# Moving the finish and the start of each FFN row group off the boundary between groups, in an eight-core decoder block

## Chip, cores and metric

The kernel runs on all 8 cores of one Trainium2 chip (two dies, cores 0 to 3 and 4 to 7). The time of a run is the device time of its slowest core, in microseconds (us). The chip has two states with this program: in some executions the cores of one die, or of both, get a lower TensorE clock and the run is several per cent longer. Such runs are called slow here; only fast runs are compared, and when a profile fell in the slow state I compare only the cores of the other die.

## The reference, cut to what matters

The model is one decoder block in float32: two kinds of sequence mixer, then a dense SwiGLU feed-forward part (FFN), each between two RMS norms. Only the FFN is touched. With `x1` the rows after the mixer:

```python
def rms_norm(x, w):
    return x * lax.rsqrt(jnp.mean(x * x, axis=-1, keepdims=True) + 1e-6) * w

# D_MODEL = 2048, D_FF = 5632; 2048 rows per core      (condensed by me)
h  = rms_norm(x1, w_pre_ffn)
ff = (silu(h @ w_gate) * (h @ w_up)) @ w_down
y  = x1 + rms_norm(ff, w_post_ffn)
```

## The kernel before

Each core works through its 2048 rows in four groups of 512. A group has a start (load four tiles of 128 rows, 1 MiB each, norm them, transpose them into `h2`), a gate and up stage (11 blocks, each with one load of `w_gate` and one of `w_up`, 2 MiB each as they land), a down stage (8 blocks with one load of `w_down` each), and a finish (norm of the result, residual load, add, store). The weights are float32 in memory and become bf16 in the load.

```python
ff = [sb(f"ff{i}", [128, D], F32, ph) for i in range(4)]      # start AND finish use these
xt = [sb(f"xq{j}", [128, D], F32, ph) for j in range(2)]
for tgi in range(NT // TG):                                   # 4 groups
    for j4 in range(4):                                       # start: load and norm
        xs, xb = ff[j4], f"ff{j4}"
        P.dma("sp", xs[:], x1d[ti * 128:(ti + 1) * 128, :], xb, r=["x1d"], w=[xb])
        P.act(junk[:], xs[:], AF.Square, ...)                 # ... root, reciprocal
        P.act(xs[:], xs[:], AF.Copy, ..., scale=...)
    for kc in range(16):                                      # start: transposes
        for j4 in range(4):
            P.tr(ps[bk][:, j4 * 128:(j4 + 1) * 128], ff[j4][:, kc * 128:(kc + 1) * 128], ident, ...)
        # eviction, 512 wide, by VectorE and ScalarE in turn:
        P.ts(h2[:, kc, :], ps[bk][:, :], wcol, None, ALU.mult, ..., w=["h2"])
    for blk in range(11):                                     # gate and up
        P.dma("pool", wslot(gsl), w_gate_v[:, :, blk * 512:(blk + 1) * 512], ...)
        P.dma("pool", wslot(usl), w_up_v[:, :, blk * 512:(blk + 1) * 512], ...)
        # ... 4 x (16 gate + 16 up matmuls), silu, product into hid
    for db in range(8):                                       # down
        P.dma("pool", dslot(ds_), w_down_v[:, :, db * 256:(db + 1) * 256], ...)
        # ... 4 x 44 matmuls, evicted into ff
    for j4 in range(4):                                       # finish
        P.dma("sp", xt[k2][:], x1d[ti * 128:(ti + 1) * 128, :], xb, r=["x1d"], w=[xb])
        # ... norm of ff[j4] (ScalarE, VectorE), then
        P.tt(xt[k2][:], xt[k2][:], ff[j4][:], ALU.add, ..., eng="pool")     # GpSimd
        P.dma("sp", y[ti * 128:(ti + 1) * 128, :], xt[k2][:], xb, r=[xb], w=["y"])
```

An eviction is the copy of a finished result out of PSUM, the memory that TensorE writes, into a tile; PSUM is used here in banks of 512 columns (`ps`).

A list scheduler orders the instructions of each engine by estimated costs when the kernel is built, and every engine then runs its list strictly in order. Waits come from tracked names: an instruction that writes a name waits for the one that wrote it before.

## Time and profile before

| | before |
|---|---|
| three timed runs | 7005.32, 6694.4, 7066.68 us (one fast, two slow) |
| profiled run | 6699.66 us, fast; cores 6653 to 6698 us |
| FFN, first gate matmul to last matmul, mean of cores | 2233.7 us |
| of it: four gate stages / four down stages / three gaps between groups | 1223.8 / 807.2 / 202.6 us |

The lower two rows are my tabulation from TensorE's timelines of all eight cores: a gate stage runs from its first to its last matmul, a down stage from the last gate matmul to the last down matmul (so the wait for its first weights is in it), the gap from the last down matmul to the next gate matmul.

### The profile page before, as it was taken

How to read it: one execution, taken by the hardware profiler on the slowest of the kernel's cores; microseconds unless marked ns; L12 is line 12 of the kernel's file. 1: busy time of each engine (PE TensorE's matmuls, PEld its weight loads, DVE VectorE, ACT ScalarE, POOL GpSimd, SP SyncE). 2: the span in 40 equal slices, each digit the busy share in tenths (PEclk: the TensorE clock that was granted, in tenths of full speed). 3: DMA queues.
4: the chain of work that ended last, by engine and by line, in shares of the span. 5: the costliest groups of instructions: out<-in, count | busy, mean ns of one | idle time of the engine just before them, and what ended most of it. 6: DMA issues, size and time to landing. Idle time of an engine off the chain costs nothing. (4 is left out here: it accounts for less than half of the span.)

```text
span 6698.1 us, 76172 instructions; the slowest of 8 cores (6653.1 to 6698.1 us)
## 1 busy us (share of the span) xinstructions
PE 4857.1 (73%) x26232; PEld 2606.6 (39%) x26232; DVE 2288.5 (34%) x4634; ACT 2138.4 (32%) x3524; POOL 361.9 (5%) x218
## 2 busy tenths in 40 slices
PE   5885788589735667565546654969859886986987
PEld 3443444344322333232222221434644473464446
DVE  1346235522731555577766541210010001001001
ACT  5631552264142545544444541220020002002000
POOL 0000000000000000000000000310010011001001
PEclk8997999699867868676668877989979998997999
DMA  5122122221023110212132344499899898988988
GB/s 128 26 44 45 76 38 41 60 73 29 13 82 73 31 36 15 49 37 61 42 70 53 79 94 103 152 168 153 107 170 144 118 127 166 155 110 164 151 117 135
DMA packets 514618, 591.83 MB, mean 88 GB/s; under 512 B 14880, under 2 KB 465568, under 8 KB 495392
## 3 DMA queue, kind: packets, MB, share of 16 engines
q0 software_dynamic: 444928, 356.66, 38.1%
q1 hardware_dynamic: 69312, 230.30, 10.8%
q8 instruction: 217, 3.56, 0.2%
q14 instruction: 161, 1.32, 0.1%
HBM read 888.77 MB, written 54.79 MB: 141 GB/s over the span
## 5 line engine op out<-in xcount | busy, mean ns | idle before, releaser
L272 PE MATMUL ps<-h_s,wr_s 128*128 128x512 bf16 x5632 | 1223.8, 381 | 12.8 <-ACT h_s L287 11.5
L272 PE MATMUL ps<-hT_s,wb_s 128*128 128x512 bf16 x2816 | 702.0, 411 | 197.5 <-DVE ub_s L315 90.1
L272 PE MATMUL ps<-hTp_s,wbp_s 128*128 128x512 bf16 x3456 | 790.5, 388 | 69.5 <-DVE ubp_s L315 30.6
L272 PEld LDWEIGHTS ps<-h_s,wr_s 128*128 128x128 bf16 x5632 | 552.5, 98 | 683.1 <-issue 24.3
L272 PE MATMUL ps<-wr_s,hid_s 128*128 128x256 bf16 x5632 | 656.8, 282 | 168.5 <-DMA wr_s<-w_down 168.5
L272 PEld LDWEIGHTS ps<-wr_s,hid_s 128*128 128x128 bf16 x5632 | 568.4, 101 | 257.8 <-issue 174.8
L272 PEld LDWEIGHTS ps<-hTp_s,wbp_s 128*128 128x128 bf16 x3456 | 342.0, 100 | 485.7 <-issue 113.3
L272 PEld LDWEIGHTS ps<-hT_s,wb_s 128*128 128x128 bf16 x2816 | 287.9, 104 | 602.1 <-issue 340.0
L296 DVE TENSOR_TENSOR hid_s<-sg_s,ps 128x512 bf16<-128x512 f32 x176 | 120.9, 687 | 1112.0 <-PE ps L272 1112.0
L287 ACT ACT_TABLE_LOAD x287 | 368.2, 1283 | 409.6 <-PE ps L272 178.0
L287 ACT ACTIVATE sg_s<-ps 128x512 f32<-128x512 f32 x176 | 105.1, 597 | 1081.9 <-PE ps L272 1081.9
L272 PE MATMUL ps<-wbp_s,hTp_s 128*128 128x512 bf16 x1536 | 358.6, 394 | 59.0 <-ACT hTp_s L287 23.2
L276 PE MATMUL ps<-cst_s,T_s 128*128 128x128 f32 (+1 forms) x1200 | 197.3, 312 | 152.5 <-ACT T_s L287 79.1
L272 PE MATMUL ps<-hT_s,mixT_s 128*128 128x512 bf16 x1024 | 223.1, 381 | 79.2 <-DMA hT_s<-w_out 79.2
L315 DVE COPY ff_s<-ps 128x256 f32<-128x256 f32 x64 | 27.1, 424 | 741.1 <-PE ps L272 741.1
L272 PEld LDWEIGHTS ps<-wbp_s,hTp_s 128*128 128x128 bf16 x1536 | 153.5, 101 | 253.9 <-issue 89.6
L314 ACT ACTIVATE ff_s<-ps 128x256 f32<-128x256 f32 x64 | 24.5, 383 | 706.6 <-PE ps L272 706.6
L287 ACT ACTIVATE T_s<-T_s 128x2048 f32<-128x2048 f32 (+1 forms) x75 | 142.9, 1905 | 296.6 <-DVE T_s L305 247.1
L276 PEld LDWEIGHTS ps<-cst_s,T_s 128*128 128x128 f32 (+1 forms) x1200 | 157.1, 163 | 192.9 <-issue 185.8
L301 DVE TENSOR_SCALAR xwt_s<-ps,wst_s 128x64 bf16<-128x64 f32 x768 | 186.0, 280 | 76.4 <-PE ps L276 47.7
L305 DVE SCALAR_TENSOR_TENSOR T_s<-ubp_s,pp_s,T_s 128x2048 f32<-128x2048 f32 x90 | 210.3, 2342 | 0.1
L276 PE MATMUL ps<-cst_s,ff_s 128*128 128x128 f32 x256 | 43.0, 324 | 205.7 <-ACT ff_s L287 199.5
(227 smaller groups left out, 5422.1 us busy)
## 6 DMA issues: line engine op xcount, KB each, us to landing
wr_s<-w_gate POOLq DMA_DIRECT2D x44, 2048.0 KB, 17.6
wr_s<-w_up POOLq DMA_DIRECT2D x44, 2048.0 KB, 25.2
wr_s<-w_down POOLq DMA_DIRECT2D x32, 2816.0 KB, 23.3
T_s<-xpre SPq DMA_DIRECT2D x48, 1024.0 KB, 9.2
wbp_s<-w_in POOLq DMA_DIRECT2D x21, 2048.0 KB, 15.1
wb_s<-w_in POOLq DMA_DIRECT2D x13, 2048.0 KB, 18.2
xt_s<-xin SPq DMA_DIRECT2D x17, 1024.0 KB, 7.0
abc_s<-acsd SPq DMA_DIRECT2D x64, 256.0 KB, 3.9
```

What stands on the lines that cost most here:

```text
L272: return self.op("pe", lambda e: e.matmul(out, lhsT, rhs, start=start, stop=stop), r, w, stop if inc is None else inc, cost=c)
L276: return self.op("pe", lambda e: e.transpose(out, in_, ident), r, w, inc, cost=110.0)
L287: return self.op(eng, lambda e: e.activation(out, in_, func, **kw), r, w, cost=c)
L296: return self.op(eng, lambda e: e.tensor_tensor(out, in0, in1, op), r, w, cost=self._dc(out, 2, eng))
L301: return self.op(eng, lambda e: e.tensor_scalar(out, in0, s1, None, op0), r, w, cost=c)
L305: return self.op("dve", lambda e: e.scalar_tensor_tensor(out, in0, scalar, in1, op0, op1), r, w, cost=self._dc(out, 2))
L314: return self.op("act", lambda e: e.activation(out, in_, AF.Copy), r, w, cost=220.0 + 0.85 * self._n(out))
L315: return self.op(eng, lambda e: e.tensor_copy(out, in_), r, w, cost=self._dc(out, 1, eng))
```

## The change

Its intent is to let TensorE go from one group's down stage straight into the next group's gate stage. Loads and norm of the next group get tiles of their own (`xa`) and run in two rounds of two row tiles under the down stage; the finish of the old group is spread over the next gate stage, one row tile at each of blocks 2, 4, 6 and 8. Three state tiles of an earlier phase are freed to make room. `u.preds` are the instructions that `u` waits for, `u.cost` is only the list scheduler's estimate of how long it takes. The diff, cut to its core:

```diff
+            xa = [sb(f"xa{j}", [128, D], F32, ph) for j in range(2)]
...
+            def post(tgi, j4, after):                      # the finish of one row tile
+                u = P.dma("sp", xt[k2][:], x1d[ti * 128:(ti + 1) * 128, :], xb, r=["x1d"], w=[xb])
+                u.preds.update(after)                       # not before these weights have landed
+                if after:
+                    u.cost = 40000.0
+                ...                                         # as before: norm, add on GpSimd, store
+            def pre_tile(tgi, rnd, jj):
+                if tgi == 0 and rnd == 0:
+                    return ff[jj], f"ff{jj}"
+                return xa[jj], f"xa{jj}"
...
             for tgi in range(NT // TG):
-                for j4 in range(4):
-                    xs = ff[j4]
+                for rnd in range(2):
+                    for jj in range(2):
+                        xs, xb = pre_tile(tgi, rnd, jj)     # load, norm as before
...
-                        P.ts(h2[:, kc, :], ps[bk][:, :], wcol, None, ALU.mult, ..., w=["h2"])
+                            o_ap = h2[:, kc, rnd * 256:(rnd + 1) * 256]      # half as wide
+                            i_ap = ps[bk][:, kk2 * 256:(kk2 + 1) * 256]
+                            if kk2 == 0:
+                                P.ts(o_ap, i_ap, wcol, None, ALU.mult, ..., w=[h2n])
+                            else:
+                                P.act(o_ap, i_ap, AF.Copy, ..., w=[h2n], scale=wcol)
...
-                    P.dma("pool", wslot(gsl), w_gate_v[...], ...)
-                    P.dma("pool", wslot(usl), w_up_v[...], ...)
+                    ug = P.dma("pool", wslot(gsl), w_gate_v[...], ...)
+                    uu = P.dma("pool", wslot(usl), w_up_v[...], ...)
+                    if tgi > 0 and blk in (2, 4, 6, 8):
+                        post(tgi - 1, blk // 2 - 1, [ug, uu])
...
-                for j4 in range(4):                         # the finish at the group's end
-                    ...
+                if tgi == NT // TG - 1:
+                    for j4 in range(4):
+                        post(tgi, j4, [])
```

More of the change, by code (lines that the diff above doesn't have):

```diff
@@ L374, in build @@
         lbc = sb("lbc", [128, 16], F32)
-        Sinb = sb("Sinb", [128, HK, 128], BF16)
-        SinA = sb("SinA", [128, 8, 128], BF16)
-        SinB = sb("SinB", [128, 8, 128], BF16)
+        sinst = ExitStack()
+        Sinb = sb("Sinb", [128, HK, 128], BF16, sinst)
+        SinA = sb("SinA", [128, 8, 128], BF16, sinst)
+        SinB = sb("SinB", [128, 8, 128], BF16, sinst)
         ps = [es.enter_context(nc.psum_tensor(f"ps{i}", [128, 512], F32)) for i in range(8)]
@@ L1226, in build @@
         mid.close()
+        sinst.close()
         with ExitStack() as ph:
@@ L1230, in build @@
             pw1 = sb("pw1", [128, D], F32, ph)
-            h2 = sb("h2", [128, 16, TG], BF16, ph)
+            h2s = [sb("h2", [128, 16, TG], BF16, ph)] * 2
             hid = sb("hid", [128, 44, TG], BF16, ph)
@@ L1235, in build @@
             xt = [sb(f"xq{j}", [128, D], F32, ph) for j in range(2)]
+            xa = [sb(f"xa{j}", [128, D], F32, ph) for j in range(2)]
             sg = [sb(f"sg{j}", [128, TG], F32, ph) for j in range(2)]
             junk = sb("junk5", [128, D], BF16, ph)
+            pjunk = [junk[:, 0:1024], junk[:, 1024:2048]]
             st = sb("st5", [128, 16], F32, ph)
+            st6 = sb("st6", [128, 16], F32, ph)
             w_gate_v = w_gate.rearrange("(k p) n -> p k n", p=128)
@@ L1248, in dslot @@
                 return wr[:, 2 * i:2 * i + 2, :].rearrange("p a b -> p (a b)")[:, 0:44 * 256].rearrange("p (f n) -> p f n", n=256)
-            for tgi in range(NT // TG):
-                for j4 in range(4):
-                    ti = tgi * 4 + j4
-                    xs = ff[j4]
-                    xb = f"ff{j4}"
-                    P.dma("sp", xs[:], x1d[ti * 128:(ti + 1) * 128, :], xb, r=["x1d"], w=[xb])
-                    ss = st[:, 4 * j4:4 * j4 + 1]
-                    P.act(junk[:], xs[:], AF.Square, r=[xb], w=["junk5", f"st5{j4}"], accum_out=ss)
-                    P.ts(st[:, 4 * j4 + 1:4 * j4 + 2], ss, 1.0 / D, EPS, ALU.mult, ALU.add, r=[f"st5{j4}"], w=[f"st5{j4}"])
-                    P.act(st[:, 4 * j4 + 2:4 * j4 + 3], st[:, 4 * j4 + 1:4 * j4 + 2], AF.Sqrt, r=[f"st5{j4}"], w=[f"st5{j4}"])
-                    P.recip(st[:, 4 * j4 + 3:4 * j4 + 4], st[:, 4 * j4 + 2:4 * j4 + 3], r=[f"st5{j4}"], w=[f"st5{j4}"])
-                    P.act(xs[:], xs[:], AF.Copy, r=[xb, f"st5{j4}"], w=[xb], scale=st[:, 4 * j4 + 3:4 * j4 + 4])
-                for kc in range(16):
-                    bk = kc % 4
-                    for j4 in range(4):
-                        P.tr(ps[bk][:, j4 * 128:(j4 + 1) * 128], ff[j4][:, kc * 128:(kc + 1) * 128], ident,
-                             r=[f"ff{j4}", "cst"], w=[f"ps{bk}"], inc=(j4 == 3))
-                    wcol = pp[:, C_PREFFN + kc:C_PREFFN + kc + 1]
-                    if kc % 2 == 0:
-                        P.ts(h2[:, kc, :], ps[bk][:, :], wcol, None, ALU.mult, r=[f"ps{bk}", "pp"], w=["h2"])
-                    else:
-                        P.act(h2[:, kc, :], ps[bk][:, :], AF.Copy, r=[f"ps{bk}", "pp"], w=["h2"], scale=wcol)
@@ new lines, in post @@
+            def post(tgi, j4, after):
+                ti = tgi * 4 + j4
+                k2 = j4 % 2
+                xb = f"xq{k2}"
+                u = P.dma("sp", xt[k2][:], x1d[ti * 128:(ti + 1) * 128, :], xb, r=["x1d"], w=[xb])
+                u.preds.update(after)
+                if after:
+                    u.cost = 40000.0
+                ss = st[:, 4 * j4:4 * j4 + 1]
+                P.act(junk[:], ff[j4][:], AF.Square, r=[f"ff{j4}"], w=["junk5", f"st5{j4}"], accum_out=ss)
+                P.ts(st[:, 4 * j4 + 1:4 * j4 + 2], ss, 1.0 / D, EPS, ALU.mult, ALU.add, r=[f"st5{j4}"], w=[f"st5{j4}"])
+                P.act(st[:, 4 * j4 + 2:4 * j4 + 3], st[:, 4 * j4 + 1:4 * j4 + 2], AF.Sqrt, r=[f"st5{j4}"], w=[f"st5{j4}"])
+                P.recip(st[:, 4 * j4 + 3:4 * j4 + 4], st[:, 4 * j4 + 2:4 * j4 + 3], r=[f"st5{j4}"], w=[f"st5{j4}"])
+                P.stt(ff[j4][:], ff[j4][:], st[:, 4 * j4 + 3:4 * j4 + 4], pw1[:], ALU.mult, ALU.mult,
+                      r=[f"ff{j4}", f"st5{j4}", "pw1"], w=[f"ff{j4}"])
+                P.tt(xt[k2][:], xt[k2][:], ff[j4][:], ALU.add, r=[xb, f"ff{j4}"], w=[xb], eng="pool")
+                P.dma("sp", y[ti * 128:(ti + 1) * 128, :], xt[k2][:], xb, r=[xb], w=["y"])
@@ new lines, in pre_tile @@
+            def pre_tile(tgi, rnd, jj):
+                if tgi == 0 and rnd == 0:
+                    return ff[jj], f"ff{jj}"
+                return xa[jj], f"xa{jj}"
+            for tgi in range(NT // TG):
+                h2 = h2s[tgi % 2]
+                h2n = "h2"
+                for rnd in range(2):
+                    for jj in range(2):
+                        j4 = rnd * 2 + jj
+                        ti = tgi * 4 + j4
+                        xs, xb = pre_tile(tgi, rnd, jj)
+                        P.dma("sp", xs[:], x1d[ti * 128:(ti + 1) * 128, :], xb, r=["x1d"], w=[xb])
+                        ss = st6[:, 4 * j4:4 * j4 + 1]
+                        P.act(junk[:], xs[:], AF.Square, r=[xb], w=["junk6", f"st6{j4}"], accum_out=ss)
+                        P.ts(st6[:, 4 * j4 + 1:4 * j4 + 2], ss, 1.0 / D, EPS, ALU.mult, ALU.add, r=[f"st6{j4}"], w=[f"st6{j4}"])
+                        P.act(st6[:, 4 * j4 + 2:4 * j4 + 3], st6[:, 4 * j4 + 1:4 * j4 + 2], AF.Sqrt, r=[f"st6{j4}"], w=[f"st6{j4}"])
+                        P.recip(st6[:, 4 * j4 + 3:4 * j4 + 4], st6[:, 4 * j4 + 2:4 * j4 + 3], r=[f"st6{j4}"], w=[f"st6{j4}"])
+                        P.act(xs[:], xs[:], AF.Copy, r=[xb, f"st6{j4}"], w=[xb], scale=st6[:, 4 * j4 + 3:4 * j4 + 4])
+                    for k2_ in range(8):
+                        bk = k2_ % 4
+                        for kk2 in range(2):
+                            kc = 2 * k2_ + kk2
+                            for jj in range(2):
+                                P.tr(ps[bk][:, (kk2 * 2 + jj) * 128:(kk2 * 2 + jj + 1) * 128], pre_tile(tgi, rnd, jj)[0][:, kc * 128:(kc + 1) * 128], ident,
+                                     r=[pre_tile(tgi, rnd, jj)[1], "cst"], w=[f"ps{bk}"], inc=(kk2 == 1 and jj == 1))
+                        for kk2 in range(2):
+                            kc = 2 * k2_ + kk2
+                            wcol = pp[:, C_PREFFN + kc:C_PREFFN + kc + 1]
+                            o_ap = h2[:, kc, rnd * 256:(rnd + 1) * 256]
+                            i_ap = ps[bk][:, kk2 * 256:(kk2 + 1) * 256]
+                            if kk2 == 0:
+                                P.ts(o_ap, i_ap, wcol, None, ALU.mult, r=[f"ps{bk}", "pp"], w=[h2n])
+                            else:
+                                P.act(o_ap, i_ap, AF.Copy, r=[f"ps{bk}", "pp"], w=[h2n], scale=wcol)
@@ L1272, in build @@
                 for blk in range(11):
                     gsl, usl = (blk % 2) * 2, (blk % 2) * 2 + 1
-                    P.dma("pool", wslot(gsl), w_gate_v[:, :, blk * 512:(blk + 1) * 512], f"wr{gsl}", w=[f"wr{gsl}"])
-                    P.dma("pool", wslot(usl), w_up_v[:, :, blk * 512:(blk + 1) * 512], f"wr{usl}", w=[f"wr{usl}"])
+                    ug = P.dma("pool", wslot(gsl), w_gate_v[:, :, blk * 512:(blk + 1) * 512], f"wr{gsl}", w=[f"wr{gsl}"])
+                    uu = P.dma("pool", wslot(usl), w_up_v[:, :, blk * 512:(blk + 1) * 512], f"wr{usl}", w=[f"wr{usl}"])
@@ L1281, in build @@
                             P.mm(ga[:, :], wslot(gsl)[:, kc, f4 * 128:(f4 + 1) * 128], h2[:, kc, :],
-                                 start=(kc == 0), stop=(kc == 15), r=[f"wr{gsl}", "h2"], w=[f"ps{k2}"])
+                                 start=(kc == 0), stop=(kc == 15), r=[f"wr{gsl}", h2n], w=[f"ps{k2}"])
                         for kc in range(16):
                             P.mm(ua[:, :], wslot(usl)[:, kc, f4 * 128:(f4 + 1) * 128], h2[:, kc, :],
-                                 start=(kc == 0), stop=(kc == 15), r=[f"wr{usl}", "h2"], w=[f"ps{2 + k2}"])
+                                 start=(kc == 0), stop=(kc == 15), r=[f"wr{usl}", h2n], w=[f"ps{2 + k2}"])
                         P.act(sg[k2][:], ga[:, :], AF.Silu, r=[f"ps{k2}"], w=[f"sg{k2}"])
@@ L1298, in build @@
                              eng=("act" if j4 % 2 else "dve"))
-                for j4 in range(4):
-                    ti = tgi * 4 + j4
-                    k2 = j4 % 2
-                    xb = f"xq{k2}"
-                    P.dma("sp", xt[k2][:], x1d[ti * 128:(ti + 1) * 128, :], xb, r=["x1d"], w=[xb])
-                    ss = st[:, 4 * j4:4 * j4 + 1]
-                    P.act(junk[:], ff[j4][:], AF.Square, r=[f"ff{j4}"], w=["junk5", f"st5{j4}"], accum_out=ss)
-                    P.ts(st[:, 4 * j4 + 1:4 * j4 + 2], ss, 1.0 / D, EPS, ALU.mult, ALU.add, r=[f"st5{j4}"], w=[f"st5{j4}"])
-                    P.act(st[:, 4 * j4 + 2:4 * j4 + 3], st[:, 4 * j4 + 1:4 * j4 + 2], AF.Sqrt, r=[f"st5{j4}"], w=[f"st5{j4}"])
-                    P.recip(st[:, 4 * j4 + 3:4 * j4 + 4], st[:, 4 * j4 + 2:4 * j4 + 3], r=[f"st5{j4}"], w=[f"st5{j4}"])
-                    P.stt(ff[j4][:], ff[j4][:], st[:, 4 * j4 + 3:4 * j4 + 4], pw1[:], ALU.mult, ALU.mult,
-                          r=[f"ff{j4}", f"st5{j4}", "pw1"], w=[f"ff{j4}"])
-                    P.tt(xt[k2][:], xt[k2][:], ff[j4][:], ALU.add, r=[xb, f"ff{j4}"], w=[xb], eng="pool")
-                    P.dma("sp", y[ti * 128:(ti + 1) * 128, :], xt[k2][:], xb, r=[xb], w=["y"])
+                if tgi == NT // TG - 1:
+                    for j4 in range(4):
+                        post(tgi, j4, [])
             P.flush()
```

## The prediction

> **What bounds the kernel now.** The change touches only the last phase, the FFN, which works through four groups of 512 rows. I read the cores' spans first (6653 to 6698 us, granted clocks 0.841 to 0.845: both dies undisturbed, so this is the fast state). Two of the three timed runs before, 7005 and 7067 us, are 5 to 6% longer than the third, 6694; I take them for the slow state and work from 6694.4 and the profiled 6699.7, so from 6,697.
>
> Next I read TensorE's waits over the FFN (engine, line, waited for: us in total, times, longest).
>
> ```profile
> PE ps L276 <- ACT ff_s L287: 199.5, 4, 53.0
> PE ps L272 <- DMA wr_s<-w_down: 168.5, 22, 21.1
> PE ps L272 <- ACT h_s L287: 11.5, 4, 3.0
> ```
>
> The first line is the transposes (L276) waiting until ScalarE has normalised the next group's rows; the second is the down projection waiting for weights. TensorE's timeline shows where they fall (start, length, instruction, idle before).
>
> ```profile
> 4869.58 40.69 PE L272 MATMUL ps<-wr_s,hid_s 128*128 128x256 bf16 x352 [6.87 <-DMA wr_s<-w_down]
> 4917.45 21.43 PE L272 MATMUL ps<-wr_s,hid_s 128*128 128x256 bf16 x176 [7.19 <-DMA wr_s<-w_down]
> 4991.78 6.60 PE L276 MATMUL ps<-cst_s,ff_s 128*128 128x128 f32 x36 [52.90 <-ACT ff_s L287]
> ...
> 5007.26 305.61 PE L272 MATMUL ps<-h_s,wr_s 128*128 128x512 bf16 x1408 [2.88 <-ACT h_s L287]
> 5332.95 41.10 PE L272 MATMUL ps<-wr_s,hid_s 128*128 128x256 bf16 x352 [20.08 <-DMA wr_s<-w_down]
> ```
>
> From the end of one down projection (4938.88) to the next gate matmul (5007.26) are 68.4 us. The same reading at the other two boundaries gives 68.0 (5526.02 to 5594.05) and 62.8 (6106.16 to 6168.99): 199.2 us in all. The gap before group 0 and the tail after group 3 (6673.2 to 6698.1) are no boundaries of this kind. The gate and up stage runs without a break, 11 blocks in 305.6 us; between its regular issues a block takes 27.65 us. The chain of waits says what fills the gap:
>
> ```profile
> 4925.16 2.01 ACT junk_s L287 x2
> 4927.50 1.28 ACT L287
> 4929.37 2.36 DVE ff_s L305
> 4931.93 4.51 POOL xq_s L296
> 4936.53 8.65 DMA y<-xq_s
> 4945.63 17.02 DMA xq_s<-x1d
> 4962.85 4.49 POOL xq_s L296
> 4967.83 13.94 DMA ff_s<-x1d
> 4981.86 2.01 ACT junk_s L287 x2
> ```
>
> The finish of the old group (norm, residual add, store) and the start of the new one follow each other because both use the four ff tiles. Twelve 1 MiB tiles move here: four stores, four residual loads, four loads to normalise. So the gap is not only latency, it is also busy with transfers. The table by windows, one stretch each for gate and up, down, the gap, and the first two blocks after it (busy by engine, granted clock, DMA share, GB/s), decides how free their new place is:
>
> ```profile
> 4535.00:4562.00 27.00, 27.00 (x127) 12.23 (x126) 2.75 (x4) 2.21 (x4) 1.69 (x2) 1.00 1.07 155
> 4752.00:4772.00 20.00, 20.00 (x174) 17.39 (x173) 0.85 (x2) 0.38 (x1) 0.00 (x0) 0.94 0.01 2
> 4939.00:5007.00 68.00, 10.99 (x64) 9.26 (x64) 13.50 (x22) 26.45 (x31) 15.49 (x5) 0.60 1.00 256
> 5007.00:5033.00 26.00, 25.74 (x113) 11.37 (x114) 2.06 (x3) 3.08 (x5) 0.00 (x0) 0.93 0.00 1
> 5034.00:5061.00 27.00, 27.00 (x127) 12.21 (x125) 2.75 (x4) 1.87 (x4) 2.08 (x2) 1.00 1.05 156
> ```
>
> The transfers are as full in the gate stage (1.05) as in the gap. They idle for the first block after a gap, because two blocks of weights landed inside it, and during the first down block (0.01). TensorE and the transfers are nearly balanced; a change that only moves transfers has little room.
>
> **What the Trainium skill says.** "DMA: Bandwidth & Descriptors", section "Issuing engines are not separate DMA queues": transfers issued by any engine end up on the same 16 DMA engines and interleave. The trace agrees: an up weight load that lands after 25 us in the gate stage took 59.9 us when issued in the gap, beside the tiles. So moving the tiles to SyncE's issue under the gate stage doesn't make them free. The same page, "Queues, rings and completion order", says that each engine takes turns between queues by packet. Here a packet of the tiles' queue averages 7.3 KB (46.02 MB in 6323), of the weights' queue 0.76 KB (276.26 MB in 361810): a tile should get through and the weights pay. "SBUF — State Buffer", section "SBUF: two separate sides", describes an exclusive port lock between VectorE with two SBUF inputs and GpSimd. The trace fits: the 128x2048 scaling took 2.35 us alone and 5.75 beside GpSimd's add. "ScalarE: Activation LUTs", section "What ACT_TABLE_LOAD costs", gives about 1283 ns for a load; the trace has 1283.
>
> **The change part by part.** (1) Loads and norm of the next group go to two new tiles (xa), in two rounds of two row tiles, and no longer need ff. The built order places round 0's 32 transposes ahead of the first down matmul, round 1's as 16 after 88 down matmuls and 16 after 88 more. The gap's 52.9 us wait for ff and the transposes after it leave the boundary. (2) The finish of the old group is spread over the next gate stage, one row tile at each of blocks 2, 4, 6 and 8, whose residual load waits until that block's weights have landed. (3) Evictions get half as wide and twice as many. Freeing the Sin tiles only makes room.
>
> Removed: 68.4 + 68.0 + 62.8 = 199.2 us.
>
> Given back in the down stage. Round 0's transposes take about 7 us (40 took 7.08 at the full rate; eviction paces them at about 0.8 us a bank) and lie inside the 20 us for which TensorE waits for the first w_down load anyway: free. At about +7 us they release xa, and two tile loads join that w_down load. A tile costs 35.7 / 12 = 2.97 us of all engines (the tile queue held 52.5% of the 68 us gap), so the first down block starts some 5.5 us later. Round 1 then needs squares, root and scaling, 4 x 2 us plus about 1.3, after loads landing near +21: ready at about +31, before 88 matmuls (10 us) are done at +36. No stall. Its 32 transposes add about 7 us on TensorE, and as the third w_down load is issued when the first down block ends, they delay it: 12.5 us so far. Then two more tile loads, for the group after next, compete with that third load. That could be 6 us; some is absorbed, as the load waits for TensorE elsewhere, so I take 2.5. Sum 15 us after groups 0 and 1, and 8 after group 2, where no such loads follow: 38 us.
>
> Given back in the gate stage. When it is backlogged, the weight pair of a block takes 26.1 us (ups landing at 4456.5, 4482.9, 4508.3 and 4534.7), so 1.55 us per block are left of 27.65. The up load lands some 3.8 us before it is needed (landed 5061.3, needed 5065). Each finished row tile moves two tiles, 5.9 us, per two blocks, against 3.1 us of room. Step by step: the lead of about 3 us leaves 1.3 us of stall at the first, then about 2.9 at each of three: 10 us per stage, in three stages 30 us. At the start of the stage the first up pair lands about 26.1 us after the last w_down load (4917.3 + 26.1 = 4943.4; needed 4938.9 + 3.6): 1 us, three times 3 us.
>
> Net: 199.2 - 38 - 30 - 3 = 128 us. 6,697 - 128 = 6,569, called 6,570: 1.9% faster.
>
> **The rivals.** (A) All hidden: the tiles run in holes of the transfers, the stage does not stall, and the down stage grows by 5 us each: 199 - 20, about 6,515. For it: the idle first block and first down block, shares of 1.16 early in group 0 without a stall. Against: that idle first block disappears with the gap that paid for it. (B) Saturated transfers: all 23.8 us of tiles in a gate stage become stalls, and GpSimd's add, which stands in the same queue ahead of block 4's weight issues, sometimes holds them back because its residual tile is late. A tile landed after 7.5 to 17 us, the add takes 4.5, and the next issue is about 24 us away: it just fits, but 5 us more per tile would cost 20 us per stage. Then 199 - 38 - 3 - 71 - up to 60: 6,610 to 6,670. (C) ScalarE in order: in the down stage the squares for the group after next stand ahead of an eviction and wait for a load, so one of two banks stays full. I work out about 5 us of stall, ending when the third w_down load lands, thus hidden; with loads of 17 us, 5 to 8 us would show twice.
>
> **Range and chances.** In the fast state I expect 6,500 to 6,650. A gain of 2% needs 134 us, 6 more than my sum, and second-order costs tend to be missed: faster 0.42, within 2% 0.56, slower 0.02. The upper end is set at 6,890, because two of three runs before were slow ones and a median may fall there; the 6,570 is meant for fast runs.
>
> **What would show it.** TensorE's 53 us waits for ff must be gone and the next gate matmul must follow the down stage within about 3 us. The down stages should be about 222, 227 and 214 us (207, 212, 206 before), the later gate stages about 316 (305.6). The waits should show w_up or w_gate with some 30 us. I am wrong if the gate stages stay at 306 (then 6,540 or less), if they pass 330, if TensorE waits for evictions or for xa, or if GpSimd's weight issues wait for an add.

## More of the kernel before

The main views are shown in the prediction. Two more are needed later. The first fence holds lines of the page of the kernel before, first its span, then three rows of its table of transfers (what is loaded from what, issuing engine, count, KB each, median us from issue to landing).

```profile
span 6698.1 us, 76172 instructions; the slowest of 8 cores (6653.1 to 6698.1 us)
...
wr_s<-w_gate POOLq DMA_DIRECT2D x44, 2048.0 KB, 17.6
wr_s<-w_up POOLq DMA_DIRECT2D x44, 2048.0 KB, 25.2
wr_s<-w_down POOLq DMA_DIRECT2D x32, 2816.0 KB, 23.3
```

The second is one row of the table by windows (length, busy time by engine, granted clock, DMA share, GB/s) over most of a gate stage, ten blocks on the slowest core.

```profile
5034.00:5310.00 276.00, 276.00 (x1281) 125.15 (x1279) 27.49 (x40) 23.67 (x40) 22.41 (x19) 1.00 1.01 148
```

TensorE is busy for all of the 276 us, and the DMA share already reads 1.01. The up load lands 25.2 us after its issue, and a block lasts 27.65. Both are close to full; whatever is added to this stage has to fit in what is left.

## The result and the profile after

| | before | after |
|---|---|---|
| median of all runs | 6977.06 us (15 runs) | 6790.1 us (12 runs) |
| fast runs | 6693.71, 6694.4, 6698.31, 6702.26 | 6583.52, 6588.98, 6592.25, 6592.8 |
| ratio of fast runs | | 0.9839, 95% interval 0.9822 to 0.9856 |

A ratio is the mean time of one kernel's fast runs over the mean of the other's fast runs of the same rounds, so it is not quite the ratio of the medians quoted beside it. The change makes fast runs 1.6% or 108 us faster. The profiled run after was fast (6592.25 us, slowest core 4).

Lines of the page after that answer to those of before:

```profile
span 6590.4 us, 76090 instructions; the slowest of 8 cores (6534.7 to 6590.4 us)
...
wr_s<-w_gate POOLq DMA_DIRECT2D x44, 2048.0 KB, 26.9
wr_s<-w_up POOLq DMA_DIRECT2D x44, 2048.0 KB, 35.3
wr_s<-w_down POOLq DMA_DIRECT2D x32, 2816.0 KB, 23.3
```

Gate and up loads take 9 to 10 us longer from issue to landing, though their number and size are the same. TensorE's waits over the FFN on core 4 (waited for: us in total, times, longest) show what that costs:

```profile
PE ps L272 <- DMA wr_s<-w_down: 160.8, 20, 23.6
PE ps L272 <- DMA wr_s<-w_up: 44.5, 13, 6.5
PE ps L276 <- ACT st_s L287: 41.8, 1, 41.8
```

The three waits of 53, 53 and 48 us at the boundaries are gone; the 41.8 us are the start of group 0, which was there before. The wait for `w_down` is as before. New is the wait for `w_up`: 44.5 us in 13 pieces. TensorE's timeline (start, length, instruction, idle before and what ended it) shows one boundary and the gate stage after it:

```profile
4938.94 20.71 PE L272 MATMUL ps<-wr_s,hid_s 128*128 128x256 bf16 x176 [5.43 <-DMA wr_s<-w_down]
4959.70 89.73 PE L272 MATMUL ps<-h_s,wr_s 128*128 128x512 bf16 x407
5051.78 55.41 PE L272 MATMUL ps<-h_s,wr_s 128*128 128x512 bf16 x251 [2.34 <-DMA wr_s<-w_up]
5112.41 57.06 PE L272 MATMUL ps<-h_s,wr_s 128*128 128x512 bf16 x251 [5.22 <-DMA wr_s<-w_up]
5171.62 55.41 PE L272 MATMUL ps<-h_s,wr_s 128*128 128x512 bf16 x251 [2.14 <-DMA wr_s<-w_up]
5230.76 50.19 PE L272 MATMUL ps<-h_s,wr_s 128*128 128x512 bf16 x219 [3.73 <-DMA wr_s<-w_up]
```

The gate stage now follows the down stage without a gap (4959.65 to 4959.70). Once per two blocks, which is once per finished row tile, TensorE waits 2 to 5 us for an up load.

On core 4 that is nearly all of it. The other cores show one more wait: about 7 us after its first matmul a stage needs its first up load, and at 14 of the 24 boundaries (three on each of eight cores) TensorE waits for it, up to 6.1 us; the means over the cores are 1.6, 2.9 and 1.9 us for groups 1, 2 and 3. On core 2, 12 us after the first matmul of the stage (4931.39):

```profile
4943.41 84.37 PE L272 MATMUL ps<-h_s,wr_s 128*128 128x512 bf16 x376 [5.16 <-DMA wr_s<-w_up]
```

The stage of core 4 by windows:

```profile
4959.70:5280.79 321.09, 306.18 (x1380) 138.27 (x1408) 34.69 (x48) 32.81 (x52) 43.09 (x25) 0.99 1.11 168
```

TensorE's busy time is 306 us, that of a whole stage before; the other 15 are waits. The transfers move 168 GB/s where they moved 148, and the DMA share reads 1.11, so the 1.01 of before was not a ceiling.

The ledger, as the mean of eight cores from TensorE's timelines ("start" is from the last matmul of the phase before to the first gate matmul):

| us | before | after | difference |
|---|---|---|---|
| start of group 0 | 59.1 | 63.5 | +4.4 |
| gate stage of group 0 | 306.5 | 306.2 | -0.3 |
| gate stages of groups 1, 2, 3 | 305.4, 305.7, 306.2 | 323.1, 325.8, 329.9 | +17.7, +20.1, +23.7 |
| down stages of groups 0, 1, 2 | 200.0, 206.4, 202.3 | 217.1, 213.9, 209.5 | +17.1, +7.5, +7.2 |
| down stage of group 3 and tail | 224.2 | 223.6 | -0.6 |
| three gaps | 202.6 | 0 | -202.6 |

The sum is -105.8 us; the mean span of the cores fell by 104.8 (6673.3 to 6568.5), since the phases before the FFN ended about 1 us later. So 202.6 us went away and 98 came back: 61.5 in gate stages, 31.8 in down stages, 4.4 at the start.

### The profile page after: what moved, and what is told of

Read it like the earlier page. It is cut to its first block, busy times and chain, and to the rows that moved or that the text cites. A ratio compares the mean times of both kernels' runs of the same rounds, so it can differ in the third digit from the quotient of the medians.

```text
span 6590.4 us, 76090 instructions; the slowest of 8 cores (6534.7 to 6590.4 us)
## 1 busy us (share of the span) xinstructions
PE 4830.9 (73%) x25887; PEld 2602.3 (39%) x26232; DVE 2283.3 (35%) x4666; ACT 2157.0 (33%) x3564; POOL 362.4 (5%) x218
## 5 line engine op out<-in xcount | busy, mean ns | idle before, releaser
L272 PE MATMUL ps<-h_s,wr_s 128*128 128x512 bf16 x5516 | 1231.2, 383 | 55.2 <-DMA wr_s<-w_up 44.5
L272 PE MATMUL ps<-hTp_s,wbp_s 128*128 128x512 bf16 x3375 | 774.6, 386 | 77.4 <-DVE xwt_s L301 30.8
L315 DVE COPY ff_s<-ps 128x256 f32<-128x256 f32 x64 | 27.2, 424 | 624.4 <-PE ps L272 624.4
L309 DVE TENSOR_TENSOR_SCAN T_s<-cst_s,T_s 128x2048 f32<-128x2048 f32 (+1 forms) x27 | 119.5, 4424 | 180.8 <-ACT T_s L287 180.5
## 6 DMA issues: line engine op xcount, KB each, us to landing
wr_s<-w_up POOLq DMA_DIRECT2D x44, 2048.0 KB, 35.3
wbp_s<-w_in POOLq DMA_DIRECT2D x21, 2048.0 KB, 15.3
```

Source lines behind the costliest of these rows:

```text
L272: return self.op("pe", lambda e: e.matmul(out, lhsT, rhs, start=start, stop=stop), r, w, stop if inc is None else inc, cost=c)
L309: return self.op("dve", lambda e: e.tensor_tensor_scan(out, d0, d1, init, op0, op1), r, w, cost=100.0 + 2.1 * self._n(out))
L315: return self.op(eng, lambda e: e.tensor_copy(out, in_), r, w, cost=self._dc(out, 1, eng))
```

## The experiments

The theory I tested, called T, is that in the gate stages each 1 MiB tile takes time from the weight loads, so that the stall is the tiles' and nothing else's. Rivals were O, the order of the matmuls (from group 1 on the built order after is gate, gate, up, up where it was gate, up, gate, up), and Q, GpSimd's in-order queue, in which the add stands ahead of the next weight issue. The trace alone speaks against Q in this kernel. These are two lines of GpSimd's timeline on core 4, the add of a row tile and the next weight issue:

```profile
5088.74 4.50 POOL L296 TENSOR_TENSOR xq_s<-xq_s,ff_s 128x2048 f32<-128x2048 f32 x1 [14.12 <-DMA xq_s<-x1d]
5094.00 1.18 POOL L328 DMA_DIRECT2D wr_s<-w_gate  x1 [0.76 <-PE ps L272]
```

After the add the issue still waits, for TensorE to free the slot (0.76 us here; 2.48, 3.22 and 0.87 at the other three of this stage). The add held nothing back, but 0.76 is a thin margin. It is the same on the other cores: in 92 of the 96 cases the issue after the add waits for TensorE, and in the other four it follows the add within 0.1 us, with the next up issue at the usual 6.9 us behind it.

"Gates" below are the stages of groups 1 to 3, "downs" those of groups 0 to 2, both as means of the cores. Experiments 1 to 4 ran on one chip, where the kernel before took 6702.99 us; the others on another, where its fast runs took 6697 to 6725 us. Every stage time is from one profiled run. The gate stage of group 0, which no edit but that of 9 and 11 touches, took 305.8 to 307.8 us in them (306.2 after), so the chips can be compared in this.

### 1. No residual loads (result wrong on purpose)

```diff
-                u = P.dma("sp", xt[k2][:], x1d[...], xb, r=["x1d"], w=[xb])
-                u.preds.update(after)
...
-                P.tt(xt[k2][:], xt[k2][:], ff[j4][:], ALU.add, r=[xb, f"ff{j4}"], w=[xb], eng="pool")
+                P.tt(xt[k2][:], ff[j4][:], ff[j4][:], ALU.add, r=[f"ff{j4}"], w=[xb], eng="pool")
```

> The changed kernel with the four residual loads of each finish left out (the scaled tile is added to itself, so the output is wrong on purpose); the stores stay, so four of the eight 1 MiB tiles per later gate stage go. Theory T (the gate stage is bound by what the 16 DMA engines move: 26.8 us per weight pair plus 3.05 us per tile, as the landings of the changed kernel give): gate stages 1 to 3 fall from 323 to 330 us (mean of 8 cores) to 308 to 313 us, so some 40 us off the whole kernel. Rival Q (GpSimd's add, waiting for its residual tile, holds back the weight issues behind it): 305 to 307 us, as the add then waits for nothing. Rival O (the other order of gate and up matmuls costs the time): unchanged, 323 to 330.

Measured: gates 317.4, 319.6, 317.9, fast run 6580.05 us. That is less than after, but more than expected. The edit changed more than I meant. Without the load that waited for weights, the finish was ready at once, and all four stores went out at the start of the stage; the stall (8.35 us for `w_up` on one core) sat in block 1 instead of being spread. A miss as a clean test of four tiles; experiment 10 does that better.

### 2. Each residual tile loaded twice

```diff
+                if after:
+                    u2 = P.dma("sp", xt[k2][:], x1d[ti * 128:(ti + 1) * 128, :], xb, r=["x1d"], w=[xb])
+                    u2.cost = 40000.0
```

> The changed kernel with every spread-out residual load done twice, one after the other into the same tile (right result): twelve tiles per later gate stage in place of eight. T: a pair of blocks needs 2 x 26.8 + 3 x 3.05 = 62.8 us against 59.7, four times: gate stages 1 to 3 at 335 to 342 us, kernel about 36 us longer. Q: the add is ready some 10 us later each time and holds the weights by 7 to 10 us: 350 us or more per stage. O: unchanged, 323 to 330.

Measured: gates 333.1, 333.5, 338.4 with 12, 12 and 14 tiles in the stage; fast run 6633.17 us, result correct. Ten more us for four more tiles in the first of them, about 8 in the others. Theory T holds, just under its range in two stages; an unchanged stage (O) and a jump past 350 us (Q) are ruled out. The kernel was 40 to 50 us longer than after, where 36 were expected; the downs had grown too (222.2, 221.5, 214.2).

### 3. The kernel before, with eight extra tile loads per gate stage

```diff
+                    if tgi > 0 and blk in (2, 4, 6, 8):
+                        for z in range(2):
+                            tz = tgi * 4 + blk // 2 - 1
+                            u = P.dma("sp", xz[z][:], x1d[tz * 128:(tz + 1) * 128, :], f"xz{z}", r=["x1d"], w=[f"xz{z}"])
+                            u.preds.update([ug, uu])
```

> The kernel before, with nothing of the change but eight dummy loads of 1 MiB tiles in each of gate stages 1 to 3 (two at each of blocks 2, 4, 6 and 8, released as in the changed kernel when that block's weights have landed; nobody reads them). T: gate stages 1 to 3 go from 306 us to 321 to 330 us, the 67 us gaps stay within 3 us, the kernel is 50 to 65 us longer (about 6750). Q and O: no add and no other order here, so gate stages stay at 306 us.

Measured: gates 320.0, 320.0, 319.3, gaps 68.1, 67.8, 67.2; fast run 6756.65 us, 54 us over the kernel before. This is the cleanest proof of T: old matmul order, no finish in the stage, no add on GpSimd, only the tiles, and the stage grows by 13 to 15 us, just under the range. In the first two stages it is 3 to 6 us less than in the kernel after, in part because here the first two blocks' weights still land in the gap: on no core does TensorE wait for a stage's first up load, where after it waits 1.6 and 2.9 us on average.

### 4. Only the first part of the change: the finish in one burst at the group's end

```diff
-                    if tgi > 0 and blk in (2, 4, 6, 8):
-                        post(tgi - 1, blk // 2 - 1, [ug, uu])
...
-                if tgi == NT // TG - 1:
-                    for j4 in range(4):
-                        post(tgi, j4, [])
+                for j4 in range(4):
+                    post(tgi, j4, [])
```

> The changed kernel with only the first part of the change: the next group is normalised ahead in its own tiles, but the finish of the old group is issued at the group's end as before, with nothing that holds it to blocks 2, 4, 6 and 8. T: the same eight tiles meet the same stream of weights, only all at the start; the gate stages 1 to 3 are 320 to 332 us as in the changed kernel, with the stall in the first two or three blocks. Rival S (the spreading is what makes the change work): tiles and adds bunched in front of the weights cost 340 us or more per stage, 30 us or more on the kernel beyond the changed one.

Measured: gates 328.8, 330.5, 338.8 (the last raised by two cores' 357 and 361); one run, 6655.86 us, in which die 0 had a slightly lower clock (0.839); the cores of the other die took 6569 to 6608 us, against 6557 to 6590 after. TensorE's timeline on core 5 at the start of a gate stage:

```profile
4958.98 8.48 PE L272 MATMUL ps<-h_s,wr_s 128*128 128x512 bf16 x32 [4.19 <-DMA wr_s<-w_gate]
4982.16 271.28 PE L272 MATMUL ps<-h_s,wr_s 128*128 128x512 bf16 x1248 [14.70 <-DMA wr_s<-w_up]
```

The whole stall comes first, then 271 us run unbroken. Spreading the finish, the second part of the change, is worth only about 5 us per gate stage: it moves the stall, it does not remove it. On the undisturbed die the FFN as a whole was 26 us longer than after (2151.3 against 2125.6 us), 12 of them in the gates and 15 in the downs, which vary by several us from run to run (see 8).

### 5. Both halves of a bank evicted by the same engine

```diff
-                            if kk2 == 0:
+                            if k2_ % 2 == 0:
```

This asks about the 4.4 us at the start. Two lines of the kernel before (VectorE, core 3), then two of the kernel after (ScalarE, then VectorE, core 3), all evictions into `h2`:

```profile
4418.48 0.75 DVE L301 TENSOR_SCALAR h_s<-ps,pp_s 128x512 bf16<-128x512 f32 x1 [0.94 <-ACT h_s L287]
4420.12 0.75 DVE L301 TENSOR_SCALAR h_s<-ps,pp_s 128x512 bf16<-128x512 f32 x1 [0.89 <-ACT h_s L287]
```

```profile
4414.58 0.47 ACT L287 ACTIVATE h_s<-ps,pp_s 128x256 bf16<-128x256 f32 x1 [0.75 <-DVE h_s L301]
4415.23 0.48 DVE L301 TENSOR_SCALAR h_s<-ps,pp_s 128x256 bf16<-128x256 f32 x1 [0.74 <-ACT h_s L287]
```

Each engine waits for the other's write, though they write different bytes. Before, two 512-wide evictions took 1.64 us; after, two 256-wide ones take about 1.25, so half the width costs three quarters of the time.

> The changed kernel with the transposed halves evicted by bank (VectorE takes both halves of one PSUM bank, ScalarE both of the next) in place of one half of every bank each. Theory H (the two halves of one bank are evicted one after the other by two engines, since the kernel's helper orders engines on a bank; each bank then costs about 1.2 us of TensorE's time in place of 0.9): the time from the last output-projection matmul to the first gate matmul falls from 63.5 us (mean of 8 cores) to 58 to 60 (59.1 before the change). Rival L (that time is set by the loads and the norm of four tiles in two rounds): it stays at 63 to 64. Gate and down stages within 3 us of the changed kernel's either way.

Measured: start 62.5 us (63.5 after); gates 323.5, 321.9, 326.8; fast run 6605.49 us. A miss: the change of engine inside a bank is not the cost. The evictions still take turns through the one tracked name.

### 6. The old matmul order

```diff
+                            if f4 > 0 or blk > 0:
+                                mg.preds.add(mu)          # a gate group after the up group before it
...
+                            mu.preds.add(mg)              # an up group after its gate group
```

> The changed kernel with gate and up matmuls forced into the order that the kernel before has (gate, up, gate, up); its own scheduler gives gate, gate, up, up from group 1 on. T: the first up weights are needed 3.5 us earlier and the gate slot is freed 3.5 us later, so a lead of 3 to 7 us is lost once per stage: gate stages 1 to 3 at 325 to 336 us (323 to 330 in the changed kernel). Rival O (the new order costs the time): 306 to 316 us.

Measured: slow (die 1 at 0.828), so only cores 0 to 3 (0.846): gates 326.4, 324.6, 334.6, against 322.7, 325.0, 328.7 on the same cores after. No gain, so O is out: the order is not what lengthens the stage.

### 7. Four of the eight tiles moved to the transfers' hole in the down stage

The two residual loads for row tiles 0 and 1 and the two stores for row tiles 2 and 3 are tied to the first 44 down matmuls, where the transfers were idle before (share 0.01 in the prediction's table).

```diff
+                        if db == 0 and j4 == 0:
+                            for jp in range(2):
+                                if tgi > 0:
+                                    ystore(tgi - 1, 2 + jp, [md])     # stores of row tiles 2, 3
+                                xload(tgi, jp, [md])                  # residuals of row tiles 0, 1
```

> The changed kernel with four of the eight tiles of each finish taken out of the gate stage and put where the transfers idle, the first block of the down stage (two residual loads of this group, two stores of the last one, released by the first down matmul group); output right. T: with four tiles left, spread out, 4 x 3.05 us against 9 us of room: gate stages 1 to 3 at 307 to 314 us (323 to 330), down stages 0 to 2 at most 5 us longer than 217, 214, 210, so 30 to 50 us off the kernel: about 6545, 0.5 to 0.8% faster than the changed kernel. Rival C (the transfer time is conserved, it only changes place): down stages longer by 10 to 12 us each, kernel within 15 us of 6590. Q: gate stages not under 318, as the adds stand in GpSimd's queue as before.

Measured: gates 317.1, 318.1, 318.9 with 4 tiles each, downs 217.5, 223.2, 212.7; one fast run, 6574.24 us. Better than after, but short of 307 to 314, and the second down stage grew by 9 us where at most 5 were expected. GpSimd's timeline on core 0 gives the reason:

```profile
5525.92 4.51 POOL L296 TENSOR_TENSOR xq_s<-xq_s,ff_s 128x2048 f32<-128x2048 f32 x1 [29.27 <-DMA wr_s<-w_up]
5530.37 1.18 POOL L328 DMA_DIRECT2D wr_s<-w_gate  x1
5531.55 1.16 POOL L328 DMA_DIRECT2D wr_s<-w_up  x1
```

My edit tied the add to weights that landed late, and both issues behind it start with no wait of their own: their slots were free, the gate's some 15 us earlier. After all 96 adds of the run the next issue follows without a wait of its own. Here rival Q is real, though it is not in the kernel after.

### 8. No finish in groups 0 to 2 (result wrong on purpose)

```diff
-                    if tgi > 0 and blk in (2, 4, 6, 8):
-                        post(tgi - 1, blk // 2 - 1, [ug, uu])
```

> The changed kernel without any finish for groups 0 to 2 (no residual load, no scaling, no add, no store: 12 of the 16 row tiles of the output are never written, wrong on purpose), so no tile crosses gate stages 1 to 3. It measures what those stages cost apart from the tiles. Theory R (the weights alone leave room, 26.7 us per block against 27.65): 305 to 308 us, as in group 0. Theory I (a stage that begins without the lead that the old gap gave is short by about 5 us whatever follows, which a line through the stages with 12 and 8 tiles suggests): 309 to 313 us.

Measured: gates 307.1, 304.0, 304.9 with no tiles; one fast run, 6562.08 us. TensorE's wait for `w_up`, on its slowest core:

```profile
PE ps L272 <- DMA wr_s<-w_up: 6.3, 2, 5.3
```

With the finish gone the gate stages are back at 304 to 307 us, so nearly all of the loss there belongs to the finish. What the missing gap itself costs is the wait for a stage's first up load, the only one left: 2.3, 0 and 0.7 us on average, 5.3 to 6.7 on four cores. But the downs became 220.0, 222.3, 218.6, that is 3, 8 and 9 us longer than after, and the FFN gained only 35 us (2088.5 against 2123.6) where the gates gave 63. The trace puts most of that in waits for `w_down` after the first down matmul, 21.4, 25.1, 22.0 and 18.6 us in the four groups against 20.5, 18.3, 15.3 and 15.0 after. The last group is among them, whose down stage no edit of the finish touches; over the runs with both dies undisturbed that stage took 197.8 to 204.5 us. So a few us in the downs are within what they vary by, and what sets these waits is open.

### 9. The halves of `h2` tracked under two names

```diff
-                            if kk2 == 0:
-                                P.ts(o_ap, i_ap, wcol, None, ALU.mult, ..., w=[h2n])
+                            if k2_ % 2 == 0:
+                                P.ts(o_ap, i_ap, wcol, None, ALU.mult, ..., w=["h2v"])
                             else:
-                                P.act(o_ap, i_ap, AF.Copy, ..., w=[h2n], scale=wcol)
+                                P.act(o_ap, i_ap, AF.Copy, ..., w=["h2s"], scale=wcol)
```

The matmuls then read both names.

> The changed kernel, evictions by bank as in e5, and VectorE's and ScalarE's evictions into h2 tracked under two names, so that one engine's eviction no longer waits for the other's last one. Theory W (each eviction waits for the one before it, as all write the one tracked name h2; 1.28 us per pair of halves, 16 pairs): the time from the last output-projection matmul to the first gate matmul falls from 63.5 us (mean) to 54 to 58, below the 59.1 of the kernel before. Rival L (loads and norm set it): 62 to 64. Stages 1 to 3 of the gate within 4 us of the changed kernel's.

Measured: start 55.3 us, so the serial writes were the cost: the only difference from 5 is the two names. Of the 8.2 us won there, 5.7 came back in the gate stage of group 0 (311.9 after 306.2), which now waits for weights. The later gates (325.0, 325.3, 338.8) and the time (6638.34 us) were disturbed in the last stage: two cores of die 0, which had a clock of 0.838, took 366 us in it (329.5 is the mean of the other die).

### 10. Four tiles in the down stage, and the add where it holds nothing back

As 7, but the add follows the first up matmuls of block 3, 5, 7 or 9 instead of the landing of weights:

```diff
+                        if tgi > 0 and blk in (3, 5, 7, 9) and f4 == 0:
+                            jp = blk // 2 - 1
+                            finish(tgi - 1, jp).preds.add(mu)
+                            if jp < 2:
+                                ystore(tgi - 1, jp, [])
```

> As e7, four of eight tiles in the down stage's hole, but GpSimd's add is released only one block later, when its tile has long landed, so that it cannot hold weight issues as it was seen to do in e7 (a gate load issued 15 us late). T with Q: gate stages 1 to 3 at 307 to 313 us (317 to 319 in e7), down stages as in e7 (217, 223, 213) or shorter; 6545 to 6560 us. If e7's stages came from the transfers alone: 316 to 319 again.

Measured: gates 312.2, 311.3, 313.3, downs 218.3, 219.9, 212.2; FFN 2093.3 us against 2123.6 after; one fast run, 6565.99 us, where I had expected 6545 to 6560. A gate stage after a boundary, on the slowest core:

```profile
4982.97 195.29 PE L272 MATMUL ps<-h_s,wr_s 128*128 128x512 bf16 x896 [5.34 <-DMA wr_s<-w_up]
```

After the wait for the first up load seven blocks run without a break. This confirms both halves of the reading of 7: four tiles cost about 7 us, and the late add had cost another 5 to 7 (the two stores tied to weights in 7 moved with the add). Of the 42 us that the gates are shorter than after, 10 came back in the downs.

### 11. Both: 10 and the two names

> e10 and e9 together, meant to beat both kernels: the sum of the two, 12 to 20 us less in the gate stages each, 6 to 9 us less at the start; 6535 to 6555 us, 2.2 to 2.5% under the kernel before.

The edit is the sum of 9 and 10. Measured: fast runs 6533.49, 6552.55 and 6556.42 us; ratio to the kernel before 0.9756 (0.9737 to 0.9776), so faster by 2.4%, result correct. Start 54.8, gates of all four groups 313.4, 312.7, 314.4, 313.0, downs 208.3, 212.7, 207.9. TensorE's waits over the FFN on core 0:

```profile
PE ps L272 <- DMA wr_s<-w_down: 85.1, 20, 20.0
PE ps L276 <- ACT xa_s L287: 68.0, 3, 23.3
PE ps L272 <- DMA wr_s<-w_up: 25.9, 11, 6.1
```

This is the version that beats both kernels; the kernel after did not run beside it, but its fast runs on the first chip took 6584 to 6593 us, and on this chip the kernel before is some 20 us slower (6713 to 6723 us). In the down stage the new order puts three quarters of the transposes ahead of the first down matmul; they wait for `xa` at the time when TensorE had waited for `w_down` anyway (29 us from the last gate matmul to the first down matmul, as in 10), and the downs are 4 to 10 us shorter than in 10. That the order is the cause is my reading; it was not tested by itself.

## Why the prediction was right or wrong

**The number.** For fast runs the text foresaw 128 us off (1.9%); 108 (1.6%) were measured, within 2% as it thought most likely, and the fast runs of 6584 to 6593 lie in its range for that state. Two steps failed. In the sum for fast runs it is the gate stage, the term "10 us per stage, in three stages 30 us" (33 with the 3 us of the junction), which measured 61.5; some 10 us of that miss and of the start's 4.4 were made good by luck, as the gaps were 3.4 us larger and the down stages 6.2 us cheaper than foreseen. The other is the base: 6570 is a fast-state time, and the median of the three timed runs before, over both states, is 7005. Read against that it says 6% faster, four times what the fast runs show, and it disagrees with the chances beside it: "work from 6694.4 and the profiled 6699.7, so from 6,697" fixed a base, and "the 6,570 is meant for fast runs" put the mismatch into words without mending it. A number that stands for a median across states needs the base of that median: 7005 less the same 128 us would have been 6877. Medians across states are also poor evidence: those of 15 and 12 runs differ by 2.7%, the fast runs by 1.6%.

**What goes.** Right: 199.2 us on one core foreseen, 202.6 as the mean of cores measured.

**The gate stage.** The mechanism was right (tiles make the weights late, TensorE waits once per finished row tile, 44.5 us for `w_up` on core 4 where "some 30" were expected), the size was not: 30 us foreseen, 61.5 measured, of which 48.4 are waits for `w_up` (mean of the cores) and 6.4 of these belong to the junction below. The failing terms are in "so 1.55 us per block are left" and "Each finished row tile moves two tiles, 5.9 us". In the first changed stage of core 4, ups landed 26.4, 26.7, 33.2, 27.2, 33.5, 26.3, 32.8, 27.1, 32.1 and 26.1 us after one another. Without tiles beside it an interval is 26.6 on average, not 26.1; with a load and a store it is 32.9, so a pair of tiles costs 6.3, not 5.9. Two blocks take 59.5 us where 58.1 were foreseen and TensorE takes 55.3, so each row tile after the first costs about 4.2 us and not 2.9 (its three waits are 5.22, 2.14 and 3.73 us). The lead absorbs part of the first stall only, as foreseen.

Two more terms were missing. First, waiting costs clock: after stalls of 2.34 and 2.14 us the next 251 recorded matmuls took 55.41 us, after one of 5.22 they took 57.06; the granted clock reads 1.00 in the 3.4 us after the first two and about 0.53 in the 3.6 us after the last. The Trainium skill, "TensorE: Matmul & The Clock Gate", section "What's actually happening", says that TensorE drops to half clock after an idle window of about 3.4 us and needs about as long at work to come back; that would lose some 1.7 us (an estimate from that figure), and the trace has 1.65. The 3.4 us are no sharp limit here, though. Over all cores, none of the 13 waits for `w_up` under 2.0 us in the changed stages was followed by matmuls at half rate (0.43 us apart in place of 0.22), 16 of the 38 from 2.0 to 3.6 us were, and all 54 above that. These 70 waits on eight cores, at 1.65 us each, come to some 14 us per core in the three stages (an estimate). Second, stage 3 held ten tiles, not eight: the residual tiles of the last group need no following gate stage, and the scheduler fetched two of them early. At the 2.6 us a tile worked out below, that is some 5 us of its 23.7.

The experiments give the curve for the first changed gate stage, before being 305.4 with none: 4 tiles 312.2 (experiment 10), 8 tiles 323.1 (after), 12 tiles 333.1 (experiment 2); with none and no gap, 307.1 (experiment 8). From 4 to 12 tiles that is 21 us for 8, or 2.6 us a tile. The first four cost 5 to 7 us, so on this line only one or two tiles are free. (In the means lie 1.6, 1.6, 0 and 2.3 us of waiting for the first up load.) The prediction's sum let 24 us of tiles cost 10.

**The down stage.** 15, 15 and 8 us foreseen, 17.1, 7.5 and 7.2 measured; the sum, 38 against 32, is close, the second group was too high. Round 0's transposes lay inside the wait for `w_down`, as worked out: the idle time before the first down matmul was 20.08 us before (core 3) and 21.67 after (core 4), with the transposes of 5280.79 to 5287.61 ahead of it. From the last gate matmul to the first down matmul it is 7.7, 6.4 and 5.9 us more than before (mean of the cores), where 5.5 were foreseen for the two loads beside the first `w_down`. The later work is 5.4, 3.2 and 3.2 us longer, where about 7 were foreseen for round 1's transposes. The groups differ most in the later waits for `w_down`: 3.8 us more in the first, 2.6 and 1.9 less in the other two. What sets those waits is open, as it is in experiment 8.

**Junction and start.** For the junction, the late first up load of a stage, 1 us at each of three boundaries was foreseen. Core 4 shows it once (1.0 us), but the mean of the cores is 1.6, 2.9 and 1.9 us, 6.4 in sum. TensorE meets this wait about 7 us inside the stage, so it stands in the gate stages of the ledger and not in the gaps, which are 0. At the start 0 was foreseen and 4.4 us were lost; the diff's third part, narrower evictions, was noted as "half as wide and twice as many" and not costed. Experiments 5 and 9 show it as serialised writes of one tracked name.

**The rivals.** A (all hidden, stages unchanged) is ruled out by the trace and experiment 3. B in its mild form (every tile paid in full) is nearer than I thought, its second half (GpSimd's add holding weights) did not occur in this kernel, and experiment 7 shows that it can. C (ScalarE in order, a bank staying full) did not show on core 4: the longest wait of a down matmul for an eviction is 0.8 us there.

## What to carry to other kernels

A boundary wait that is also full of transfers can't simply be hidden: ask where its bytes go, and take the stage's free room from the interval between backlogged loads set against TensorE's time per block, not from how seldom TensorE waits now. Put moved transfers where the trace shows idle DMA engines (about half of the tiles moved into the down stage gave back some 30 us of the FFN), and check what stands ahead of the load issues in the same in-order queue. Half-width instructions that write one tracked name in turn cost three quarters as much as full ones, and a number compared with a median of fast and slow runs must be built on that same median.

## What the Trainium skill lacked or had wrong

- "DMA: Bandwidth & Descriptors", section "Bandwidth", gives 6.15 us (341 GB/s) for 1 MB alone, and no rate for loads that cast float32 to bf16, nor for a tile beside them. Here a backlogged pair of such loads (4.19 MB as bf16) landed every 26.6 us, which is 158 GB/s as written; a 1 MiB tile beside them landed 8.3 to 10.6 us after its issue and cost the weights about 3.1 us, or 2.2 to 2.6 us of the stage.
- No page gives a figure for how much one queue's transfers delay another's. Here the median up load went from 25.2 to 35.3 us to landing beside the tiles, and gate stages with 4, 8 and 12 tiles took 312, 323 and 333 us.
- "TensorE: Matmul & The Clock Gate", section "What's actually happening", gives an idle window of about 3.4 us for the drop to half clock, and nothing for a single shorter wait. Here waits of 2.0 to 3.6 us were followed by half rate in 16 of 38 cases, longer ones in 54 of 54, shorter ones in none of 13.
